# Moving the SBUF buffers of a two-layer transformer block: activations at multiples of 256 bytes, weights 64 bytes past one

## The chip, the cores and the metric

The kernel runs on one core of one Trainium2 chip. The metric is the device time of one execution in microseconds (us), the median of three runs. The engines are named as in the profile: PE is TensorE's matmul, PEld its weight load, DVE is VectorE, ACT is ScalarE, POOL is GpSimd, SP is SyncE, which here only issues transfers.

## The reference

Two layers of a block with 256 tokens of width 1024, all in float32. Each layer projects the normed input by a matrix of 8004 columns, runs three kinds of attention (differential softmax, stick-breaking, and softmax over the 64 best keys), weighs their outputs by sigmoid gates, and adds the result to x; then an MLP with 4096 hidden columns and a gated projection of a side input p follow.

```python
for i in range(DEPTH):                      # DEPTH = 2
    h = rmsnorm(x, attn_norm[i])
    proj = h @ w_in[i]                      # 1024 x 8004
    (aq, ak, av, bq, bk, bv, cq, ck, cv, iq, ik, iw, gl) = jnp.split(proj, offsets, axis=-1)
    ...                                     # y_a, y_b, y_c: three attentions
    merged = (gates[:, :, 0] * (y_a @ w_br_a[i]) + gates[:, :, 1] * (y_b @ w_br_b[i])
              + gates[:, :, 2] * (y_c @ w_br_c[i]))
    x = x + merged @ w_out[i]
    hm = rmsnorm(x, mlp_norm[i])
    x = x + jnp.square(jax.nn.relu(hm @ w_up[i])) @ w_down[i]
    hp = rmsnorm(x, ple_norm[i])
    x = x + jax.nn.sigmoid(hp @ w_ple_gate[i]) * (p[i] @ w_ple_proj[i])
```

## The kernel before

**Three matmuls for one product.** Each float32 factor is split into a high part and the rest, both of the type fp32r: `wh` and `wl` for weights, `xh`/`xl` or `yh`/`yl` for activations. `mm3` (L399) issues three matmuls for each product: high by high, high by low, low by high.

**Weights.** `load_unit` (L380) brings 256 rows of a weight matrix as a tile `w` of [128, 2, 512] with one transfer from SP's queue, then ACT copies it to `wh` and DVE (sometimes POOL) subtracts to get `wl`. There are 4 buffers of `w` and 6 each of `wh` and `wl`, 4096 bytes a partition each.

**Two forms of product.** `chunk_T` (L429, through `T_steps`, L419) holds 128 columns of weights stationary and moves 256 tokens of the activations past them: matmuls of 256 columns. A chunk of 512 output columns with 1024 inputs is 96 such matmuls, on two halves `fp` of a PSUM tile `mmp`. It serves bq and bk, the six gate chunks `gl`, the branch products, w_out, w_up, and the ple products of layer 0. `down` accumulates w_down's product the same way in four PSUM halves `acc`. `chunk` (L404) does it the other way round: the activations of 128 tokens stationary, the weights move, 512 columns wide (324 for idx). It serves the q, k and v projections of attention a and c, bv, idx and the ple products of layer 1.

**Activations.** `Norm` (L470) makes `xh`/`xl`, [128, 8, 256] each, the input of all products behind a norm. For the norm ahead of the attention and of the MLP they have one buffer each from `small`; for the ple norm (`spare`) they take two of the four `g8` buffers, which otherwise hold the gates and the q and k of attention. `acts4` (L324) makes `yh`/`yl`, [128, 4, 256], the input of the branch products, w_out, w_down and the ple projection. `t2k`, `big` and `small` (L312 to L319) hand out the rest: temporaries of 2 and 4 KB, rows and columns.

**Order.** `Program` records all operations and `schedule` sorts each engine's list by a model of costs and due times; all operations then carry one source line, L293, in the trace, so that tiles tell them apart. `STREAM` (L51) gives the order of a layer's projections and attentions; in the MLP, `up(c)` and `down(c - 1)` alternate.

**Pools.** All SBUF tiles come from three pools that lie one behind the other: `cp` for constants, `wp` for the three weight tiles, `sp` for all else, each tile behind the one before in the order in which the code first asks for it.

Of the kernel before, what the change touches and what calls it, by code (L numbers as in the profile page):

```python
# [296 lines left out]
def hybrid_block(ctx: ExitStack, tc: tile.TileContext, I, out):  # L297
    nc = tc.nc
    prog = Program(nc)
    V, S, G, T, Q = (prog.engine(e) for e in ("DVE", "ACT", "POOL", "PE", "SP"))  # L300

    cp = ctx.enter_context(tc.tile_pool(name="cp", bufs=1))
    wp = ctx.enter_context(tc.tile_pool(name="wp", bufs=6))
    sp = ctx.enter_context(tc.tile_pool(name="sp", bufs=2))
    pmm = ctx.enter_context(tc.tile_pool(name="pmm", bufs=2, space=PSUM))
    ptr = ctx.enter_context(tc.tile_pool(name="ptr", bufs=2, space=PSUM))
    psc = ctx.enter_context(tc.tile_pool(name="psc", bufs=2, space=PSUM))

    def const(name, shape, dt=F32):
        return prog.tile(cp, shape, dt, name)  # L310

    def t2k(name, cols=512):  # L312
        return prog.tile(sp, [P, cols], F32, name, tag="t2", bufs=T2, ahead=AHEAD_T2)
# [2 lines left out]
        return prog.tile(sp, shape, dt, name, tag="big", bufs=5, ahead=AHEAD_BIG)  # L316

    def small(name, shape, bufs, dt=F32, tag=None):
        return prog.tile(sp, shape, dt, name, tag=tag or name, bufs=bufs)  # L319

    def g8(name, dt=F32):
        return prog.tile(sp, [P, 8, SEQ], dt, name, tag="g8", bufs=4)
# [37 lines left out]
    load_x(1)  # L360
    prog.fixed = -LEAD_LOAD + GAINS_AFTER
    pos_i = const("pos_i", [P, NB], I32)
    Q.dma_start(out=pos_i, in_=I["positions"].rearrange("o (b p) -> p (o b)", p=P), allow_slow_non_contiguous=True)

    GAINS = ("", "idx_k_norm", "a_k_norm", "c_k_norm", "a_q_norm", "c_q_norm")
    gains = const("gains", [P, len(GAINS), DEPTH, HD])
    for i, n in enumerate(GAINS):
        if n:
# [68 lines left out]
    def rsqrt_mean(ss, n, width):  # L437

        ms = small("ms", [P, 8], 4)
        V.tensor_scalar(ms[:, :n], ss, 1.0 / width, EPS, op0=OP.mult, op1=OP.add)  # L440
        r = small("rsq", [P, 8], 10)
        G.tensor_tensor(out=r[:, :n], in0=ms[:, :n], in1=half[:, :n], op=OP.pow)
        return r[:, :n]
# [26 lines left out]
    class Norm(Acts):  # L470
# [3 lines left out]
        def __init__(self, gains, spare=False):  # L474
            if spare:
                super().__init__([(g8("xh", FR), g8("xl", FR))])
            else:
                super().__init__([tuple(small(n, [P, 8, SEQ], 1, FR) for n in ("xh", "xl"))])
            self.gains = gains
            self.ss, self.made_row = None, None  # L480
# [77 lines left out]

    first_table = S.preload_act_table_set("trig_and_small")
    ncol0, ncol = const("ncol0", [P, 8]), const("ncol", [P, 50])  # L560

    def columns(src, dst):
# [37 lines left out]
    inv = const("inv", [P, 32])  # L600
# [30 lines left out]
    identb = const("identb", [P, P], BF)  # L631
    mA = const("mA", [P, NB, NB * P], BF)
    mB = const("mB", [P, P], BF)
    negone_r, ntri_r = const("negone_r", [P, P], FR), const("ntri_r", [P, P], FR)
# [489 lines left out]
```

## Time and profile before

| | before |
|---|---|
| time, median of 3 runs | 995.71 us (994.51 to 998.32) |
| profiled execution: time | 993.37 us |
| profiled execution: span | 991.7 us |
| PE busy | 977.0 us (99%), 7506 matmuls |
| DVE busy | 654.2 us (66%) |
| ACT busy | 540.6 us (55%) |
| POOL busy | 154.7 us (16%) |
| moved by DMA | 168.59 MB, mean 170 GB/s |

The span is the time from the first to the last instruction that was profiled. Matmuls overlap: one starts before the one ahead has ended, and their ends are modelled, so "mean ns of one" of a matmul is longer than the time that it takes from the stream. That time, the pitch, is read from starts: from two rows of the timeline, or from a piece of the chain of waits, in which a run of matmuls stands with its length and count.

### The profile page before, as it was taken

To read this page: it belongs to the slowest core of one execution; us is meant where nothing else is said; L and a number is where in the kernel's file an instruction comes from. 1 tells how busy PE (TensorE), PEld (TensorE's weight loads), DVE (VectorE), ACT (ScalarE), POOL (GpSimd) and SP (SyncE) were. 2 spreads that over 40 slices of the span, in tenths; PEclk is the share of its full clock that TensorE was granted. 3 is DMA by queue.
4 is the path that set the end of the run, shared out by engine and by line. 5 is a ranking of instruction groups with operands and counts; after the bars stand their busy time and mean duration, and the time that the engine had idled before them with its cause. 6 is when DMAs were issued, how large, how long until landed. Compare 5 with 4: busy or idle time off the path is not lost.

```text
span 991.7 us, 18465 instructions
## 1 busy us (share of the span) xinstructions
PE 977.0 (99%) x7506; PEld 923.5 (93%) x7506; DVE 654.2 (66%) x1009; ACT 540.6 (55%) x770; POOL 154.7 (16%) x137
## 2 busy tenths in 40 slices
PE   8899999999999999999999999999999999999998
PEld 7888889899999999999989788898999999999997
DVE  8748997754776545557676599875557755555573
ACT  7447674475455444556564576645745545554462
POOL 1202223214220000001321102330152100000010
PEclk9999999999999999999999999999999999999999
DMA  8664345635656565556456543555265665566551
GB/s 274 196 204 130 93 152 159 185 115 176 194 171 204 180 195 187 171 180 208 150 162 185 171 134 113 166 169 173 86 210 166 186 204 171 177 195 201 193 172 43
DMA packets 89194, 168.59 MB, mean 170 GB/s; under 512 B 5722, under 2 KB 9236, under 8 KB 89108
## 3 DMA queue, kind: packets, MB, share of 16 engines
q1 hardware_dynamic: 89108, 167.40, 54.1%
q8 instruction: 59, 0.97, 0.4%
q14 instruction: 27, 0.22, 0.1%
HBM read 166.33 MB, written 1.05 MB: 169 GB/s over the span
## 4 chain that ended last, share of the span: by engine, by line
PE 94%; DVE 3%; ACT 2%; DMA 0%; issue 0%; SPq 0%; POOL 0%; ACTq 0%; DVEq 0%
PE mmp L293 68%; PE acc L293 18%; PE z L293 2%; PE sc L293 2%; PE oc L293 1%; DVE qo L293 1%; PE qps L293 1%; ACT wh L293 1%; PE ob L293 1%; DVE wl L293 1%; PE pps L293 1%; DVE io L293 1%; DMA w<-in_w_in 0%; PE xps L293 0%; DVE rm L293 0%
## 5 line engine op out<-in xcount | busy, mean ns | idle before, releaser
L293 ACT ACTIVATE wh<-w 128x1024 fp32r<-128x1024 f32 (+2 forms) x318 | 331.0, 1045 | 217.0 <-PE mmp L293 107.6
L293 DVE TENSOR_TENSOR wl<-w,wh 128x1024 fp32r<-128x1024 f32 (+1 forms) x284 | 342.2, 1213 | 154.9 <-ACT wh L293 149.8
L293 PE MATMUL mmp<-xh,wh 128*128 128x256 f32 x1088 | 310.4, 285 | 2.7 <-DVE rm L293 2.7
L293 PE MATMUL mmp<-xh,wl 128*128 128x256 f32 x1088 | 309.7, 285 | 0.0
L293 PE MATMUL mmp<-xl,wh 128*128 128x256 f32 x1088 | 308.7, 284 | 0.0
L293 PEld LDWEIGHTS mmp<-xh,wh 128*128 128x128 f32 x1088 | 208.1, 191 | 5.0 <-issue 4.0
L293 PEld LDWEIGHTS mmp<-xh,wl 128*128 128x128 f32 x1088 | 208.0, 191 | 1.2 <-issue 1.0
L293 PEld LDWEIGHTS mmp<-xl,wh 128*128 128x128 f32 x1088 | 208.0, 191 | 0.4
L293 PE MATMUL acc<-yh,wh 128*128 128x256 f32 x512 | 141.7, 277 | 0.0
L293 PE MATMUL acc<-yl,wh 128*128 128x256 f32 x512 | 141.4, 276 | 0.0
L293 PE MATMUL acc<-yh,wl 128*128 128x256 f32 x512 | 141.4, 276 | 0.0
L293 POOL TENSOR_TENSOR wl<-w,wh 128x1024 fp32r<-128x1024 f32 x34 | 84.0, 2470 | 214.3 <-ACT wh L293 214.3
L293 PE MATMUL mmp<-wh,xh 128*128 128x512 f32 (+2 forms) x296 | 113.1, 382 | 0.7 <-ACT av L293 0.7
L293 PE MATMUL mmp<-wh,xl 128*128 128x512 f32 (+2 forms) x296 | 112.0, 380 | 0.0
L293 PE MATMUL mmp<-wl,xh 128*128 128x512 f32 (+2 forms) x296 | 111.5, 378 | 0.0
L293 PEld LDWEIGHTS acc<-yl,wh 128*128 128x128 f32 x512 | 96.2, 188 | 0.0
L293 PEld LDWEIGHTS acc<-yh,wh 128*128 128x128 f32 x512 | 96.2, 188 | 0.0
L293 PEld LDWEIGHTS acc<-yh,wl 128*128 128x128 f32 x512 | 96.1, 188 | 0.0
L293 PE MATMUL mmp<-yl,wh 128*128 128x256 f32 x336 | 93.0, 278 | 0.2
L293 PE MATMUL mmp<-yh,wh 128*128 128x256 f32 x336 | 93.0, 277 | 0.2 <-ACT pp L293 0.2
L293 PE MATMUL mmp<-yh,wl 128*128 128x256 f32 x336 | 92.8, 277 | 0.0
L293 POOL TENSOR_TENSOR rsq<-ms,half 128x8 f32<-128x8 f32 (+3 forms) x30 | 47.0, 1572 | 224.2 <-DVE ms L293 224.2
(196 smaller groups left out, 1205.2 us busy)
## 6 DMA issues: line engine op xcount, KB each, us to landing
w<-in_w_in SPq DMA_DIRECT2D x118, 512.0 KB, 3.9
w<-in_w_up SPq DMA_DIRECT2D x64, 512.0 KB, 3.7
w<-in_w_down SPq DMA_DIRECT2D x64, 512.0 KB, 4.4
w<-in_w_out SPq DMA_DIRECT2D x16, 512.0 KB, 4.4
w<-in_w_ple_gate SPq DMA_DIRECT2D x16, 512.0 KB, 3.7
w<-in_w_br_a SPq DMA_DIRECT2D x8, 512.0 KB, 5.1
w<-in_w_br_c SPq DMA_DIRECT2D x8, 512.0 KB, 3.6
w<-in_w_br_b SPq DMA_DIRECT2D x8, 512.0 KB, 4.3
```

Of the source, the lines that this page charges most:

```text
L293: getattr(self.engines[op.eng], op.name)(*op.args, **op.kw)
```

## The change

The same tiles are asked for in the same order with the same sizes, but out of eight pools instead of three, so that they lie elsewhere. Tiles whose size is a multiple of 2048 bytes stay in `sp`, other multiples of 256 bytes go to `mp`, the little ones to `lp`, behind all. Four constants stay ahead of the weights, and between the pools stand little buffers that shift what follows: `m8` (two of 32 bytes) ahead of the weights, `ms` and `iw` (four of 32, two of 16 in 32) behind them.

```diff
     cp = ctx.enter_context(tc.tile_pool(name="cp", bufs=1))
+    gap0 = ctx.enter_context(tc.tile_pool(name="gap0", bufs=1))
     wp = ctx.enter_context(tc.tile_pool(name="wp", bufs=6))
+    gap1 = ctx.enter_context(tc.tile_pool(name="gap1", bufs=1))
     sp = ctx.enter_context(tc.tile_pool(name="sp", bufs=2))
+    mp = ctx.enter_context(tc.tile_pool(name="mp", bufs=1))
+    lp = ctx.enter_context(tc.tile_pool(name="lp", bufs=1))
+    gaps = dict(m8=gap0, ms=gap1, iw=gap1)
...
+    def pool_for(shape, dt):
+        size = math.prod(shape[1:]) * mybir.dt.size(dt)
+        return sp if size % 2048 == 0 else mp if size % 256 == 0 else lp
+
     def const(name, shape, dt=F32):
-        return prog.tile(cp, shape, dt, name)
+        first = ("identb", "negone_r", "ntri_r", "inv")
+        return prog.tile(cp if name in first else pool_for(shape, dt), shape, dt, name)
...
     def small(name, shape, bufs, dt=F32, tag=None):
-        return prog.tile(sp, shape, dt, name, tag=tag or name, bufs=bufs)
+        return prog.tile(gaps.get(name) or pool_for(shape, dt), shape, dt, name, tag=tag or name, bufs=bufs)
```

Every engine's list of instructions, its waits included, is the same before and after, instruction for instruction; the addresses differ. This is where the tiles start in a partition, in bytes, as the two programs lay them out. The buffers of one tile follow each other at multiples of 1024 bytes, and the slices that a matmul takes (a kt, a block of 128 or 512 columns) start at multiples of 512 bytes within them, so a tile's remainder by 256 is that of all its slices.

| tiles | before: start, remainder by 256 | after: start, remainder by 256 |
|---|---|---|
| `w`, `wh`, `wl` | 32320 to 97856, 64 | 18496 to 84032, 64 |
| `t2` buffers (qo, rm, aT, pT, ur, ...) | 97856 on, 64 | 84224 on, 0 |
| `xh`, `xl` (attention and MLP norm) | 110144 and 118336, 64 | 104704 and 112896, 0 |
| av, bv, cv | 134144 on, 0 | 121088 on, 0 |
| `big` buffers (p, be, bsh, ba, ...) | 146624 on, 192 | 129280 on, 0 |
| `g8` buffers (gates, q and k, the ple norm's `xh`, `xl`) | 167104 on, 192 | 149760 on, 0 |
| `yh`, `yl` | 203008 to 227584, 0 | 182528 to 207104, 0 |
| xT | 20384, 160 | 96512, 0 |
| ident | 16512, 128 | 16512, 128 |
| identb, negone_r, ntri_r | 192 | 0 |

## Rows read from the trace of the kernel before

**Rows 1.** The page, parts 1 and 2: busy us, share, instructions; granted clock
```profile
PE 977.0 (99%) x7506; PEld 923.5 (93%) x7506; DVE 654.2 (66%) x1009; ACT 540.6 (55%) x770; POOL 154.7 (16%) x137
PEclk9999999999999999999999999999999999999999
```

**Rows 2.** Waits of PE, longest first: us in total, times, longest us
```profile
PE mmp L293 <- DVE rm L293: 2.7, 1, 2.7
PE ips L293 <- DVE io L293: 1.6, 1, 1.6
...
PE mmp L293 <- ACT pp L293: 0.2, 1, 0.2
```

**Rows 3.** PE groups by form: out<-in, shapes, count | busy us, mean ns | idle
```profile
L293 PE MATMUL mmp<-xh,wh 128*128 128x256 f32 x1088 | 310.4, 285 | 2.7 <-DVE rm L293 2.7
...
L293 PE MATMUL acc<-yh,wh 128*128 128x256 f32 x512 | 141.7, 277 | 0.0
...
L293 PE MATMUL mmp<-wh,xh 128*128 128x512 f32 x248 | 98.4, 397 | 0.0
...
L293 PE MATMUL mmp<-yh,wh 128*128 128x256 f32 x336 | 93.0, 277 | 0.2 <-ACT pp L293 0.2
...
L293 PE MATMUL oc<-pT,cv 128*64 128x128 f32 x96 | 13.0, 279 | 0.0
L293 PE MATMUL mmp<-wh,xh 128*128 128x324 f32 x32 | 10.3, 321 | 0.7 <-ACT av L293 0.7
...
L293 PE MATMUL oa<-av,aT 128*128 128x128 f32 x48 | 6.3, 274 | 0.0
```

**Rows 4.** Chain of waits in the MLP: start us, us, what, count
```profile
334.15 10.90 PE acc L293 x96
345.05 11.50 PE mmp L293 x96
356.56 10.90 PE acc L293 x96
...
923.51 11.50 PE mmp L293 x96
935.01 10.90 PE acc L293 x96
```

**Rows 5.** Chain of waits, w_out of layers 0 and 1, last down chunk
```profile
267.94 18.13 PE mmp L293 x160
...
756.93 18.14 PE mmp L293 x154
...
946.35 10.92 PE acc L293 x96
```

**Rows 6.** Windows: stretch, us, each engine's busy us and count, clock, DMA share, GB/s
```profile
268.00:284.00 16.00, 16.00 (x144) 16.00 (x143) 11.30 (x14) 7.51 (x12) 4.86 (x4) 1.00 0.54 162
757.00:773.00 16.00, 16.00 (x138) 16.00 (x137) 10.42 (x13) 7.85 (x12) 4.82 (x4) 1.00 0.53 154
...
480.00:496.00 16.00, 16.00 (x137) 16.00 (x136) 10.16 (x14) 8.77 (x13) 3.90 (x4) 1.00 0.47 140
...
80.00:150.00 70.00, 69.15 (x498) 60.59 (x497) 65.28 (x141) 49.39 (x87) 13.08 (x7) 1.00 0.43 130
```

**Rows 7.** Timeline of PE, 512 columns: start us, us, what; settled, last ple projection, unsettled
```profile
60.63 0.39 PE L293 MATMUL mmp<-wh,xl 128*128 128x512 f32 x1
...
61.76 0.39 PE L293 MATMUL mmp<-wl,xh 128*128 128x512 f32 x1
...
960.53 0.40 PE L293 MATMUL mmp<-wl,yh 128*128 128x512 f32 x1
...
961.45 0.39 PE L293 MATMUL mmp<-wh,yl 128*128 128x512 f32 x1
...
102.11 0.40 PE L293 MATMUL mmp<-wh,xh 128*128 128x512 f32 x1
...
103.04 0.39 PE L293 MATMUL mmp<-wl,xh 128*128 128x512 f32 x1
```

**Rows 8.** DVE groups by form, as rows 3
```profile
L293 DVE TENSOR_TENSOR yl<-ur,yh 128x512 fp32r<-128x512 f32 x32 | 22.0, 689 | 3.4 <-ACT yh L293 3.4
...
L293 DVE TENSOR_TENSOR gate<-gate 128x512 f32<-128x512 f32 x16 | 11.2, 717 | 0.1
```

**Rows 9.** PE groups from 80 to 150 us, as rows 3
```profile
L293 PE MATMUL mmp<-xh,wh 128*128 128x256 f32 x68 | 19.5, 287 | 0.0
L293 PE MATMUL mmp<-xh,wl 128*128 128x256 f32 x67 | 19.3, 289 | 0.0
L293 PE MATMUL mmp<-xl,wh 128*128 128x256 f32 x67 | 19.1, 285 | 0.0
```

## Prediction

> **What bounds the kernel now.** I read the page's first parts, then the chain of waits, then the pitch of single matmuls. TensorE is busy for 977.0 of 991.7 us at the full clock [rows 1], and its waits on other engines, ten rows from 2.7 us down to 0.2, come to about 10 us [rows 2]. So the time is the number of matmuls times their pitch, the time from one matmul's start to the next's; the "mean ns of one" of a group is no pitch, since matmuls overlap. Most of the work is two kinds of 256-column matmul that differ only in the activations that move: xh/xl (3 x 1088) and yh/yl (3 x 512 into acc, 3 x 336 into mmp) [rows 3]. The chain of waits gives their pitch without any model of ends. In the MLP the two alternate, 96 at a time, with no wait between: 96 with xh/xl take 11.50 us, 96 with yh/yl 10.90 us [rows 4]. That is 119.8 against 113.5 ns, in the same stage, with the same weights buffers, shapes and neighbours, and the chain repeats it in every one of the pieces of 96 shown.
>
> The layout table above has one thing that sets them apart: the start modulo 256. Weights lie at 64. yh/yl lie at 0. xh/xl lie at 64, with the weights. The change puts xh/xl where yh/yl lie, relative to the weights and also in absolute remainder, and leaves yh/yl and weights as they are. So the trace of before already holds the layout of after, in 2544 matmuls, and I price from those.
>
> **The phase.** One thing spoils a flat price. In the w_out product yh/yl move in both layers, with the same remainders. In layer 0, 160 matmuls take 18.13 us, 113.3 ns each; in layer 1, 154 take 18.14 us, 117.8 ns each [rows 5]. Windows of 16 us say the same: 144 against 138 matmuls, of which some 2 are in flight at the edge [rows 6]. All that I see to differ is the moment at which PE came out of the wait ahead. So at the remainders 0 and 64 there are two steady states, which I call A (113.3) and B (117.8); a restart picks one, and it stays until the next break. Of three restarts after a wait that I can follow on yh/yl, two fell into A (that at 267 us, and the last down chunk, 96 acc in 10.92 us) and one into B [rows 5].
>
> **The change, part by part.** No instruction, wait or transfer is added, removed or reordered; only addresses change, so queues and schedule stay.
>
> MLP, w_up: 768 matmuls a layer with xh/xl, 1536 in all. In state A each saves 119.8 - 113.5 = 6.25 ns: 9.6 us. After the change nothing switches the remainders between up and down, so I expect each MLP to keep the state that its first up chunk finds; I take A.
>
> Gates and bq/bk: 16 chunks of 96, 1536 matmuls, cut up by the attention matmuls, so with many restarts. I take A two times in three, as counted above: 2/3 x 6.25 + 1/3 x (119.8 - 117.8) = 4.8 ns, 7.4 us.
>
> The ple gate of layer 0: 192 matmuls with xh/xl in g8 buffers, at 192 now. 137 in 16 us, less the 2.4 in flight, is 118.9 ns [rows 6]; to 113.5 that saves 5.4 ns: 1.0 us.
>
> Chunks with the activations stationary and the weights moving (some 840 matmuls, [rows 3] has the main forms). The weights stay at 64, the stationary xh/xl go from 64 to 0. Now the settled pitch is 1.13 us over 5, 226 ns [rows 7]. The layout of after (64 moving, 0 stationary) stands once, in the last ple projection: 0.92 us over 4, 230 ns; but that is right behind a transpose, where chunks at today's remainders are not settled either (0.93 us over 4, 232 ns) [rows 7]. Bounds: 230 - 226.7 = 3.3 ns dearer on about 680, +2.2 us; or the same gain as the others, 6.25 ns on 840, -5.3 us. I take 0, since behind a break the two layouts are alike.
>
> Plain fp32 matmuls of attention: oc and oa get equal remainders (0 and 0). If they then paid what xh/xl pay now: 144 x 6.25 ns [rows 3] = 0.9 us. I take 0: other pairs, aqk and cqk among them, stay at equal remainders as they are.
>
> VectorE, ScalarE and GpSimd instructions read and write the moved tiles. A VectorE op with both inputs in SBUF at equal remainders (gate with gate) takes 717 ns, one at 64 and 0 (ur with yh) 689 or less [rows 8]. The latter becomes equal: 30 ns on a few dozen, on an engine that is busy 66% of the span [rows 1]. Nothing on the path. The weights' own splits keep their addresses, and so do the transfers of w.
>
> Where PE's gain could be eaten: from 80 to 150 us VectorE is busy 65.28 of 70 us [rows 6]. About 202 of the matmuls with xh/xl lie there [rows 9], worth 202 x 6.25 = 1.3 us a layer, and VectorE's 4.7 us of slack covers that on the mean though not at each point. I take 0.5 us off for both layers.
>
> Sum: 9.6 + 7.4 + 1.0 - 0.5 = 17.5 us. The profiled execution took 993.37 us, so 975.9; the median of the runs is 995.71, so 978.2. I predict **978 us**.
>
> **The rule that speaks against it.** The rows say that the same matmul takes 119.8 or 113.5 ns by where its moving operand lies [rows 4]. The Trainium skill, "SBUF — State Buffer", section "Who interferes with whom", gives TensorE two independent read ports, one for the moving operand and one for loading weights, and says that PE never waits on anyone. By that the two reads could not meet and the layout would be free: the sum would be 0 and the time 995.7 us. The trace doesn't bear it out as far as the remainder is the cause; that the cause is another is the second rival.
>
> **Rivals.** (1) *A phase lock in B.* One of the two MLPs, restarted after its norm, falls into B and keeps it for up and down. Then its 768 up matmuls save 2.0 instead of 6.25 ns, and its 768 down matmuls, now at 113.5, go to 117.8: 3.3 + 3.3 = 6.6 us lost, 984.8 us; both MLPs 991.4. For it: one restart in three, and that B held for 154 matmuls. Against it: every entry from up to down in the MLP's pieces of 96 [rows 4] ends in A.
> (2) *The difference is not the remainder.* xh/xl and weights both lie in the lower half of SBUF, yh/yl in the upper, and that stays so. If that were the cause, nothing would change: 995.7 us. Against it: the g8 buffers lie in the upper half too, and their matmuls take 118.9 [rows 6], not 113.5.
> (3) *The chunks with moving weights gain as well*, to the lower bound above: 972.9 us. For it only symmetry; against it the 230 ns.
> (4) *The other side: B everywhere.* If at 0 and 64 B is the rule once nothing at equal remainders resets the phase between up and down, the 3264 matmuls with xh/xl save 2.0 ns (-6.5 us), and the 2373 with yh/yl that are in A now (2544 less the some 170 of that w_out stretch) pay 4.3 ns (+10.2 us); with the +2.2 us of moving weights that is +5.9, 1001.6 us. It decides from the point where about three quarters of all these matmuls are in B (20.4 us of gain in A, less 2.2, against 13.9 + 10.2 that full B takes back). Against it: about 7% of those with yh/yl are now.
>
> **How the numbers follow.** Forecast 56% (its own range 974 to 982: all restarts in A give -20.2 us, 975.5; half of those in the gates in B and another 1 us lost to VectorE give 980.3; a us or so either side for the run); one MLP in B 22%, both 4%; moving weights gain 8%; not the remainder 7%; slower 3%. The range 971 to 988 holds the forecast, one MLP in B and the gain of (3), 86%, less their tails. A measurement tells about 0.5%, 5 us, from no change: faster holds the forecast, one MLP in B and (3), 0.87; same holds both in B, (2) and what lies between, 0.10; slower 0.03.
>
> **What would show it.** In the chain of after, the MLP's 96 up matmuls at 10.9 us like the 96 down ones: right. Up at 11.3 and down at 11.3: B. Up still at 11.5: the remainder isn't the cause, and the prediction falls. In windows of the gate chunks, 141 to 144 matmuls in 16 us where there is no break. Moving weights: pitch 226 ns in the av and cq chunks, if it is neither 230 nor 220. VectorE's and ScalarE's busy sums should stay within 1%, PE's waits about 10 us; if these grow to over 15 us, the gain went to VectorE in the attention stage.

## The result, and the profile after

The changed kernel takes 980.23 us (median of 4 runs, 978.46 to 980.81) where the kernel before, on the same chip, takes 996.71: a ratio of 0.9833, with a 95% interval of 0.9808 to 0.9858. A later set of runs on one chip gave 980.95 against 995.37, 0.9854 [0.9831, 0.9878]. The forecast was 978, with a range of 971 to 988.

The profiled execution took 980.81 us, with a span of 979.0. The chain of waits in the MLP, as in [rows 4] (start us, us, what, count):

```profile
310.16 10.88 PE acc L293 x96
321.04 10.88 PE mmp L293 x96
331.92 10.88 PE acc L293 x96
342.80 10.88 PE mmp L293 x96
...
824.73 10.88 PE mmp L293 x96
835.61 10.88 PE acc L293 x96
```

The 96 up matmuls, 11.50 us before, now take what the 96 down ones take: 10.88 us, 113.3 ns each, in both layers. That is state A (113.3 ns), up and down alike.

The gate and projection stages look different. Windows of the kernel before, then of the one after, in which gate and bq/bk chunks run, the first without a break, the second with a break of eight transposes (columns as in [rows 6]):

```profile
40.00:55.00 15.00, 15.00 (x128) 15.00 (x127) 8.09 (x11) 6.66 (x7) 2.41 (x1) 1.00 0.59 176
150.00:160.00 10.00, 10.00 (x87) 10.00 (x86) 7.88 (x19) 4.21 (x7) 4.90 (x3) 1.00 0.45 131
```

```profile
40.00:55.00 15.00, 15.00 (x130) 15.00 (x129) 8.23 (x11) 6.60 (x8) 2.41 (x1) 1.00 0.57 176
150.00:160.00 10.00, 10.00 (x88) 10.00 (x87) 8.03 (x19) 4.59 (x6) 4.90 (x3) 1.00 0.47 146
```

130 matmuls in 15 us, less the 2.4 in flight at the edge, is 117.6 ns: state B (117.8). In state A it would be 134 or 135. The same at 150 us, where A would give 91. So here the change gave 2 ns a matmul, not 6.

Two stretches of the profiled execution of after ran at half the clock, 1.2 GHz (the third number from the end is the granted clock: 0.50, and a mean of 0.83 over the 10 us, that is 3.4 us at half). First the kernel before, then after:

```profile
32.80:36.20 3.40, 3.40 (x31) 3.40 (x30) 2.56 (x9) 0.68 (x2) 0.56 (x1) 1.00 0.78 206
466.00:476.00 10.00, 8.79 (x75) 8.38 (x74) 8.15 (x13) 7.09 (x12) 6.05 (x6) 1.00 0.57 189
```

```profile
32.80:36.20 3.40, 3.40 (x19) 3.40 (x18) 2.24 (x8) 0.00 (x0) 0.55 (x1) 0.50 0.77 243
466.00:476.00 10.00, 8.78 (x59) 8.33 (x58) 5.84 (x9) 4.56 (x8) 3.85 (x2) 0.83 0.56 169
```

Both stand behind a wait that PE has in the kernel before as well (2.6 us for rm, 1.1 for ssum), where the clock stayed up in that execution. Each costs about half its 3.4 us. The layout does not decide whether they come: the second profile of the changed kernel has the first stretch and not the second, and the mean granted clock of single runs lay between 0.994 and 1.000 for the kernel before and between 0.996 and 1.000 for the changed one. Of the kernel before the run at 1.000 was the fastest (992.4 us), one at 0.994 the slowest (998.37). The profile of before caught a clock of 0.999, that of after 0.996, which makes some 3 us. So the two profiled executions are only 12.6 us apart (993.37 and 980.81), while the medians are 14.4 and 16.5 apart.

### The profile page after: what moved, and what is told of

The parts are those of the page before. It is cut to its first block, busy times and chain, and to the rows that moved or that the text cites. A ratio compares the mean times of both kernels' runs of the same rounds, so it can differ in the third digit from the quotient of the medians.

```text
span 979.0 us, 18465 instructions
## 1 busy us (share of the span) xinstructions
PE 964.5 (99%) x7506; PEld 909.6 (93%) x7506; DVE 654.6 (67%) x1009; ACT 539.1 (55%) x770; POOL 154.8 (16%) x137
## 4 chain that ended last, share of the span: by engine, by line
PE 92%; DVE 3%; ACT 2%; DMA 2%; issue 1%; SPq 0%; POOL 0%; ACTq 0%; DVEq 0%
PE mmp L293 66%; PE acc L293 18%; PE z L293 2%; PE sc L293 2%; PE oc L293 1%; DMA w<-in_w_in 1%; DVE qo L293 1%; PE qps L293 1%; ACT wh L293 1%; DVE wl L293 1%; PE ob L293 1%; PE pps L293 1%; DVE io L293 1%; DMA xin<-in_x 0%; DVE rm L293 0%
## 5 line engine op out<-in xcount | busy, mean ns | idle before, releaser
L293 PE MATMUL mmp<-xh,wh 128*128 128x256 f32 x1088 | 306.4, 282 | 2.6 <-DVE rm L293 2.6
L293 PE MATMUL mmp<-xh,wl 128*128 128x256 f32 x1088 | 305.5, 281 | 0.0
L293 PE MATMUL mmp<-xl,wh 128*128 128x256 f32 x1088 | 304.6, 280 | 0.0
L293 PEld LDWEIGHTS mmp<-xl,wh 128*128 128x128 f32 x1088 | 205.7, 189 | 0.4
```

The costliest lines, as they stand in the source:

```text
L293: getattr(self.engines[op.eng], op.name)(*op.args, **op.kw)
```

## The experiments

**All activations at 64, with the weights.** One buffer of 64 bytes more between the weights and the activations, in the new pools (seven in SBUF, not the eight of the section on the change):

```diff
+    pad = gap1.tile([P, 16], F32, name="pad")
     gaps = dict(m8=gap0, ms=gap1, iw=gap1)
```

> The changed kernel with 64 more bytes between the weights and the activations, so that in its new pools all activations (xh, xl, yh, yl and the rest) lie at 64 by 256, as the weights do; nothing else moves. If the distance of activations and weights makes the pitch: all 5808 matmuls of 256 columns at 119.8 ns as xh/xl were before, the chunks with moving weights back at 226.7 ns: about 995 us + 2544 x 6.3 ns = 1011 us. If the gain came from the new pools or the place in the lower or upper half: about 980 us, pitch 113.3 ns in the MLP.

Measured: 1009.48 us, ratio to before 1.0144 [1.0123, 1.0165]. The chain in the MLP:

```profile
326.63 11.52 PE mmp L293 x96
338.15 11.52 PE acc L293 x96
349.67 11.52 PE mmp L293 x96
```

Both kinds now take 120.0 ns. 64 bytes alone move the kernel by 29 us, and yh/yl, which were quick in the kernel before, became as slow as xh/xl were. So neither the new pools nor the half of SBUF in which a tile lies matters: the second rival falls.

**Weights at 0, activations at 192.** The distance of the changed kernel, with other absolute remainders; `m8` goes from ahead of the weights to the little tiles:

```diff
-    gaps = dict(m8=gap0, ms=gap1, iw=gap1)
+    gaps = dict(ms=gap1, iw=gap1)
```

> The changed kernel with m8 moved from ahead of the weights to the little tiles behind all: weights at 0, activations at 192, so activations minus weights is -64 as in the changed kernel, but no activation lies at a multiple of 256. If the distance decides: 980 us, MLP pitch 113.3 ns, moving weights 229 to 233 ns. If the moving operand's own multiple of 256 decides: 256-column matmuls at 118 to 120 ns, moving weights (now at 0) faster by up to 6 ns: about 1000 us, between 995 and 1010.

Measured: 981.57 us, ratio 0.9859 [0.9834, 0.9883]. No activation lies at a multiple of 256 bytes, and the gain is there: it is the distance from the weights that counts, not the activations' own remainder. Its six runs fall into two sets, though: four from 979.99 to 982.14, and two of 988.43 and 988.91. The profile is of one of the latter, and its chain shows why. Layer 0, then layer 1:

```profile
323.75 11.31 PE mmp L293 x96
335.06 11.31 PE acc L293 x96
346.36 11.31 PE mmp L293 x96
```

```profile
811.10 10.88 PE mmp L293 x96
821.98 10.88 PE acc L293 x96
832.86 10.88 PE mmp L293 x96
```

11.31 us for 96 is 117.8 ns. Layer 0's MLP sits in state B, up and down alike, from 298 us until transposes break in ahead of the last down chunk, at 459; layer 1's is in A. This is the first rival as it was described, in a kernel of the same distance. It was priced at 6.6 us, and the two sets lie about 7.5 apart. In this profile the branch products and w_out of layer 0 are in B as well; which chunks are in A in the four quicker runs is not shown, since none of them was profiled.

**Only xh and xl of the two norms back at 64.** They lie right behind the weights; all else as in the changed kernel:

```diff
+    xp = ctx.enter_context(tc.tile_pool(name="xp", bufs=1))
     gap1 = ctx.enter_context(tc.tile_pool(name="gap1", bufs=1))
...
-                super().__init__([tuple(small(n, [P, 8, SEQ], 1, FR) for n in ("xh", "xl"))])
+                super().__init__([tuple(prog.tile(xp, [P, 8, SEQ], FR, n, tag=n, bufs=1) for n in ("xh", "xl"))])
```

> The changed kernel with only xh and xl of the attention and MLP norms put back to 64 by 256 (right behind the weights); all other activations stay at 0. If these two tiles carry the gain: w_up and gate pitch 119.8 ns again, 994 to 997 us, the gain all gone (the ple gate's 192 matmuls stay as in the changed kernel). If other tiles carried a part, it stays: under 990 us.

Measured: 994.23 us, ratio 0.9994 [0.9982, 1.0005]. The chain is that of the kernel before:

```profile
324.60 11.50 PE mmp L293 x96
336.10 10.90 PE acc L293 x96
```

The gain is gone within what these runs tell, so it hangs on these two tiles of 8 KB a partition. Moving every other activation tile from 64, 192 or 160 to 0 is worth less than 2 us by the interval.

**The pitch by itself.** Kernels of bare matmuls, with the operands' starts as data. The block is left out; out is a copy of x.

```python
for name, form, m, s, brk in CASES:       # start remainders of activations and weights; length of the break
    ...                                   # per step: high by high, high by low, low by high
    nc.tensor.matmul(out=t[:, 0:n], lhsT=st[:, a:a + 128], rhs=mv[:, b:b + n], ...)
    ...
    nc.scalar.activation(junk[:, 0:brk], t[:, 0:brk], AF.Copy)   # PE waits for this before the next group
```

> Not the block: only matmuls of fp32r data on SBUF tiles, in the same triple pattern, at chosen start remainders; out holds x. Groups of 24 matmuls of 256 columns (activations move, names T) and of 12 of 512 columns (weights move, names C), each group 8 times, each behind a break of another length. Letters a to h: activations minus weights 0, 32, ... 224 with the weights at 64; p: 64 and 0, q: 0 and 192, r: 128 and 0, s: 192 and 0 (activations, weights). If the distance decides: Ta 120 ns settled, Tg 113.3 or 117.8, Ts as Tg, Tp and Tq alike (+64), Tr as Te, some 119 ns; Cg 229 to 233, Ca 226.7, Cs as Cg, Cp as Cc. If the moving operand's own remainder decides: Tq as Tg at 113, Tp as Ta at 120, Ts as Te at 119, and all C of letters a to h alike.

Groups by form, x192 in eight groups of 24, x96 in eight of 12; all have the same tail of a group in their busy time, so the differences come from the pitch, that of the first, unsettled matmuls of a group included:

```profile
L248 PE MATMUL Ta<-X,W 128*128 128x256 f32 x192 | 25.0, 286 | 3.4 <-ACT junk L251 3.1 <-ACT junk L229 0.3
L248 PE MATMUL Te<-X,W 128*128 128x256 f32 x192 | 24.9, 285 | 3.5 <-ACT junk L251 3.5
L248 PE MATMUL Tq<-X,W 128*128 128x256 f32 x192 | 24.8, 284 | 3.5 <-ACT junk L251 3.5
...
L248 PE MATMUL Ts<-X,W 128*128 128x256 f32 x192 | 24.3, 283 | 3.5 <-ACT junk L251 3.5
...
L248 PE MATMUL Tg<-X,W 128*128 128x256 f32 x192 | 24.3, 282 | 3.5 <-ACT junk L251 3.5
L248 PE MATMUL Cg<-W,X 128*128 128x512 f32 x96 | 24.2, 401 | 3.5 <-ACT junk L251 3.5
L248 PE MATMUL Ca<-W,X 128*128 128x512 f32 x96 | 24.1, 399 | 3.5 <-ACT junk L251 3.5
```

The settled pitch is read from starts, over the last nine matmuls of a group (six in the wide form). Two groups of Tg, for example, with the starts nine matmuls apart: 1.06 us, 117.8 ns each, in the first, and 1.02 us, 113.3 ns, in the second:

```profile
42.74 0.52 PE L248 MATMUL Tg<-X,W 128*128 128x256 f32 x3
...
43.80 0.28 PE L248 MATMUL Tg<-X,W 128*128 128x256 f32 x1
...
85.14 0.50 PE L248 MATMUL Tg<-X,W 128*128 128x256 f32 x3
...
86.16 0.28 PE L248 MATMUL Tg<-X,W 128*128 128x256 f32 x1
```

Mean of the eight groups:

| activations minus weights | 256 columns, activations move | 512 columns, weights move |
|---|---|---|
| 0 (a) | 120.0 ns | 227.1 ns |
| 32 (b) | 117.7 | 233.1 |
| 64 (c; p; q) | 117.8; 117.2; 117.8 | 233.3; 233.3; 233.3 |
| 96 (d) | 120.0 | 234.6 |
| 128 (e; r) | 118.5; 118.6 | 233.0; 232.6 |
| 160 (f) | 117.3 | 233.3 |
| 192, that is -64 (g; s) | 114.4; 115.0 | 228.9; 228.9 |
| 224 (h) | 118.2 | 233.3 |

Two pairs at one distance and other absolute remainders (c with p and q, g with s) agree to a ns, and q, whose activations start at a multiple of 256, is at 117.8. So the distance decides; a period other than 256 bytes was not tried. Of the multiples of 32, -64 is the best when activations move. When the weights move, 0 is, at 226.7 settled in seven of eight groups, and -64 costs 2 ns. (In these wide groups the second and third matmul of a product stand the other way round than in the kernel.) At -64 the groups are in A or B: 11 of 16 settle at 113.3, 5 at 117.8. That is a third, in the same matmuls on the same addresses; what differs between the groups of one layout is what stands ahead of them, the group before and its break. At 64 one group of 24, of p, settled at 113.3 too.

**High and low parts apart.** The same, with xh, xl, wh and wl each at a remainder of its own, all 64 combinations of multiples of 64, and eight layouts in which both activations lie 16, 48, ... 240 past both weights, for both forms; bare matmuls again, in the kernel's order.

> Only matmuls again (out holds x): 256 columns, activations moving, with the high and the low parts each at a remainder of their own. Name Tabc: xh at 64 a, xl at 64 b, wl at 64 c (a = 0, b = 64, c = 128, d = 192), wh at 0; four groups of 24 each. Tna to Tnh: both activations 16, 48, ... 240 past both weights. If only the distance of what moves to what is loaded for the next matmul counts: Tdda (today's -64) 113.3 or 117.8, Taaa 120, and a layout in which each moving operand is 64 below the weights that load beside it (xh below wh, xl below wl) stays at 113.3 to 117.8; nothing gets below 113.3. If the state B comes from the repeated wh of the triple, some layout with xl or wl set apart shows 113.3 in all four groups.

> As the run with names T, for 512 columns with the weights moving and the activations stationary, three groups of 12 each, names C. If the distance alone counts: Caaa 226.7, Cdda (today's) 228.9, most others 233 ns. A layout that is at 113.3 to 114.4 in its T form and at 226.7 here would beat the changed kernel by some 840 x 2.3 ns, 2 us; if none is, the changed kernel's distance is the best for the sum.

```profile
L344 PE MATMUL Tddc<-X,W 128*128 128x256 f32 x96 | 12.1, 282 | 1.7 <-ACT junk L347 1.7
L344 PE MATMUL Tnd<-X,W 128*128 128x256 f32 x96 | 12.1, 281 | 1.8 <-ACT junk L347 1.8
L344 PE MATMUL Tdda<-X,W 128*128 128x256 f32 x96 | 12.1, 282 | 1.6 <-ACT junk L347 1.6
```

| layout (xh, xl, wl relative to wh) | 256 columns, each of four groups | 512 columns, mean |
|---|---|---|
| dda: 192, 192, 0 (the changed kernel) | 117.8, 113.3, 113.3, 113.3 | 228.8 ns |
| ddc: 192, 192, 128 | 113.3, 113.3, 113.3, 113.3 | 230.9 |
| nd: 112, 112, 0 | 113.3, 113.3, 113.3, 113.3 | 233.3 |
| aaa: 0, 0, 0 | 120.0, 120.0, 120.0, 120.0 | 228.6 |

No layout gets below 113.3. Two show it in all groups: wl set 128 bytes on, and a distance of 112. Two parts of the expectations failed. Layouts in which xh lies 64 below wh and xl 64 below wl were to stay at 113.3 to 117.8, if only what moves beside the load of the next weights counted; dda did, but dab, dbc and dcd settled at 118.4 to 120.0. And with 512 columns most layouts were to settle at 233 ns; only some 15 of 72 did, and most of the others lie between 228.6 and 232.5. In the kernel's order the wide form costs about the same at -64 (228.8) as at 0 (228.6, with 226.7 in one group of three). No layout is best in both forms. The bare sum of 5808 narrow and 840 wide matmuls is 852 us for ddc, 854 for nd and 857 for dda with one group in four in B, so ddc was tried.

**The better layout in the kernel.** `wl` alone moves to 192; the `ms` buffers, 128 bytes, go between `wh` and `wl`, so nothing is added:

```diff
+    gapm = ctx.enter_context(tc.tile_pool(name="gapm", bufs=1))
+    wlp = ctx.enter_context(tc.tile_pool(name="wlp", bufs=6))
     gap1 = ctx.enter_context(tc.tile_pool(name="gap1", bufs=1))
...
-    gaps = dict(m8=gap0, ms=gap1, iw=gap1)
+    gaps = dict(m8=gap0, ms=gapm, iw=gap1)
...
-        lo = prog.tile(wp, [P, 2, n], FR, "wl", tag="wl", bufs=6, padded_shape=[P, 2, 512])
+        lo = prog.tile(wlp, [P, 2, n], FR, "wl", tag="wl", bufs=6, padded_shape=[P, 2, 512])
```

> The changed kernel with wl alone moved on by 128 bytes, to 192 by 256 (the ms buffers lie between wh and wl; w and wh stay at 64, activations at 0). If the settled pitches of the bare matmuls carry over (113.3 ns in all four groups there, against 117.8 in one of four at the changed kernel's layout; wide ones 230.9 against 228.8 ns): all xh/xl and yh/yl stretches settle at 113.3, which takes some 5 us from the gate and bq/bk chunks, and the 840 matmuls with moving weights cost 1.7 us more: about 977 us, with little scatter between runs. If the state is picked by something else than the addresses of high and low parts: as the changed kernel, 980 us, or 2 us above it.

> The changed kernel as it is, once more on the same chip. 978 to 981 us if both MLPs find state A; single executions 6 to 7 us longer if one MLP falls into B (pitch 117.8 ns for up and down alike), which no run of it has shown so far, while the kernel with weights at 0 and activations at 192, of the same distance, did in two of six.

Measured: 977.20 us (977.15 to 978.75), ratio 0.9818 [0.9798, 0.9839], against 980.95 (980.30 to 981.56) for the changed kernel on the same chip. The windows of the gates and of bq/bk that the kernel after had in state B, in this kernel, then in the second profile of the changed one:

```profile
40.00:55.00 15.00, 15.00 (x134) 15.00 (x133) 8.21 (x11) 6.76 (x8) 2.41 (x1) 1.00 0.58 176
150.00:160.00 10.00, 10.00 (x91) 10.00 (x90) 8.26 (x19) 4.68 (x7) 4.90 (x3) 1.00 0.49 140
```

```profile
40.00:55.00 15.00, 15.00 (x130) 15.00 (x129) 7.62 (x11) 6.11 (x8) 2.41 (x1) 1.00 0.58 176
150.00:160.00 10.00, 10.00 (x91) 10.00 (x90) 8.28 (x19) 4.88 (x7) 4.90 (x3) 1.00 0.50 149
```

134 and 91 matmuls in place of 130 and 88: state A. On this chip all its runs are quicker than all of the changed kernel and of the one before, and the time is the 977 us expected. The terms came out otherwise than expected, though, from starts to starts against the changed kernel's second profile: the gates, bq/bk and the ple gate gained 2.2 us (212.26 to 210.05) where some 5 had been put, w_out of layer 1, in B in that profile, 0.8, and the moving weights cost nothing on the sum (177.0 to 176.6), since two of the changed kernel's chunks had settled at 232 and 233 ns, against one here at 234. At 150 us the changed kernel finds A in one profile and B in the other, at 40 us B in both.

## Why the prediction held, point by point

The predicted sum was -17.5 us; the profiled pair gave -12.6, after some 3 lost to the stretches at half clock, and the medians -14.4 and -16.5. The time lies 2.2 us from the forecast. Two terms were put too well, by 2.6 and 1.4 us, and 0.8 us that was not in the sum made up a part of it, by luck. Term by term, from starts to starts in the two profiles:

- *The MLP, 9.6 us: right.* The up matmuls went from 184.6 to 174.8 us for both layers, 9.7. Both MLPs were in A in both profiles of this kernel, and the times of its eight runs, 978.46 to 981.56, leave no room for the 6.6 us of B. That it could have been B is not idle: the experiment with weights at 0 shows nearly a whole MLP in it.
- *Gates, bq/bk and the ple gate, 8.4 us: the mechanism right, the size off.* Their matmuls with xh/xl went from 217.0 to 213.8 us, 3.2. Without the matmuls next to a break and those at half clock their mean fell from 119.6 to 116.0 ns, 5.8 us, where two thirds in A would have given 114.8: the count of restarts, three, was small, and some places in the program find B each time (at 40 us in both profiles of after). The two stretches at half clock took about 2.4 back. The sign of 141 to 144 matmuls in 16 us failed there: 130 in 15 us are 138 in 16. The ple gate settled in B in this profile, at 118 after 119 ns, and in A in the second.
- *Moving weights, 0 with bounds of -5.3 and +2.2: it was +1.4.* They settle at 229 ns in most chunks, as in these two rows, twelve matmuls and 2.75 us apart, and at 233 in one:

```profile
164.82 0.39 PE L293 MATMUL mmp<-wh,xl 128*128 128x512 f32 x1
...
167.57 0.39 PE L293 MATMUL mmp<-wh,xl 128*128 128x512 f32 x1
```

Before, nearly all settled at 226.7. Here the one place with the later layout (230 ns, [rows 7]) was the better guide than the zero I took; I had put it down to the transpose ahead. The second profile has +2.4.

- *Not in the sum: w_out of layer 1*, in B before, was in A: 0.8 us gained, the same kind of luck the other way. In the second profile it is in B again.
- *oc and oa, 0: right.* From starts to starts they take 12.2 and 6.0 us before and after, although both operands now have equal remainders.
- *VectorE eats 0.5: no sign of more.* PE's waits sum to 10.1 us, 10.3 before. Nor does VectorE mind equal remainders: ur with yh, both at 0 now, takes 688 ns, 689 before [rows 8], so the remainder is not what sets gate with gate apart:

```profile
L293 DVE TENSOR_TENSOR yl<-ur,yh 128x512 fp32r<-128x512 f32 x32 | 22.0, 688 | 3.4 <-ACT yh L293 3.4
...
L293 DVE TENSOR_TENSOR gate<-gate 128x512 f32<-128x512 f32 x16 | 11.2, 718 | 0.1
```

- *The rivals.* The cause is the remainder (the first two experiments), the wide ones lose a little, and B is not the rule at this distance.

The measured terms, 9.7 + 5.8 - 1.4 + 0.8, are 14.9 us at full clock; less some 3 at half clock they come near the 12.6 of the profiled pair.

As to the Trainium skill's rule that PE never waits on anyone ("SBUF — State Buffer", "Who interferes with whom"): these runs measure 113.3 to 120.0 ns for one matmul by nothing but the distance of its two SBUF operands, so the layout is not free, as I had read that rule to say. What in the hardware makes the distance count stays open. That the read of the moving operand meets the load of the next weights is not shown, and in its simplest form it does not fit: the layouts dab, dbc and dcd were to be quick by it and took 118.4 to 120.0 ns.

## What to carry to other kernels

Where PE is busy all the time, read the pitch of equal matmuls on different tiles from the chain of waits: if two tiles of one type and shape differ, compare their start addresses before looking for a wait. A layout that exists already elsewhere in the same kernel prices the change, and a short kernel of bare matmuls over many remainders can find a better one in a single run: here one that was quick after all four breaks tried. Compare profiles only at the same granted clock: two stretches of half clock hid some 3 us here.

## What the runs showed of the hardware that I had not expected

At one and the same layout a stream of matmuls has two steady pitches, 113.3 and 117.8 ns, and keeps the one that it starts with for up to 160 us (layer 0's MLP with weights at 0). The place of the low weights matters too: moving only wl by 128 bytes, with wh, xh and xl kept, removed the slower state in all four groups of bare matmuls and in the windows of the kernel shown. The bare matmuls whose weights move took 2 ns more by it (228.8 to 230.9).
